# Early weight slices in tiles of their own, two transposes moved into the first feed-forward unit, and a shifted raw weight buffer

## The chip, the cores and the metric

The kernel runs on one core of a Trainium2 chip. The metric is device time in microseconds. Five engines work side by side, each strictly in the order of its own instruction list: TensorE (PE; its weight loads are listed as PEld), VectorE (DVE), ScalarE (ACT), GpSimd (POOL) and SyncE (SP), which here only issues transfers. A semaphore makes an instruction wait for one on another engine. A program places the instructions of each engine at build time, so the lists are fixed before the kernel runs.

## The reference

One transformer block on 512 positions and 2048 columns, all in float32:

```
h   = rmsnorm(x, g_attn_pre);  p = h @ w_in          # 512x2048 @ 2048x3904
o_A = stick_breaking_attention(q, k, v)              # 8 heads x 128
o_B = mla_attention(...)                             # 8 heads, low-rank q and kv
x   = x + rmsnorm(concat(rmsnorm(o_A), rmsnorm(o_B)) @ w_o, g_attn_post)
h   = rmsnorm(x, g_ffn_pre)
u   = causal_conv3(h @ w_up)                         # 2048 x 2*5632
x   = x + rmsnorm((gelu(u_gate) * u_val) @ w_down, g_ffn_post)
```

## The kernel before

Each float32 matrix is split into a high and a low part, and each product is three matmuls: high by high, high by low, low by high. A weight slice therefore passes four places: a transfer issued by SP brings it into a raw tile `wr`, ACT casts it to `wh` (L109), DVE subtracts to `wl` (L111), and TensorE reads both. Up to the feed-forward part, `load_w` (L104 to L112) does this with two raw tiles, `wr`, and four each of `wh` and `wl`.

The work around the change is at about a third of the span.

**The product with w_o.** Its columns go in four blocks of 512. Blocks c = 0, 1, 2 are done for all four row blocks of 128 positions at once (from L718). The last block is done row block by row block: `last_cols(ws, t)` (L738) is 48 matmuls of 128x512 over eight weight slices `ws`. The first four of these slices, and the first two of w_up (each 512 KB), are loaded ahead by `early_w` (L844). Its high and low parts go to pages that the feed-forward part needs only later, `a5h`, `a5l`, `a6h`, `a6l` for w_o and `a3h`, `a3l` for w_up; its raw tiles come from the same two as those of `load_w`:

```python
    def early_w(src, tag, shape):
        raw_ = new_raw(shape)
        sy.dma_start(raw_, src.rearrange("(k p) c -> p k c", p=P))
```

**The end of a row block.** After `last_cols(t)`, `residual(t)` (L779) forms the second norm and scales: DVE adds the residual (L784), ACT squares (L786), DVE sums (L754, L755), POOL raises to the power -1/2 (L757, `r`), DVE and ACT scale into `v` and `y` (L791, L793). Then `transposed(t)` (L798) turns the row block over: 16 TensorE transposes of 128x128 into four banks (L801), DVE scales each bank into a page (L803), ACT casts to `act_hi` (L774) and DVE subtracts to `act_lo` (L775). The columns of `act_hi` and `act_lo` are the positions: row blocks 0 and 1 are `lo_half`, 2 and 3 `hi_half`. In the code before, `transposed(t - 1)` stands behind `last_cols(t)`, and `transposed(3)` behind the gate's lower half.

**The first feed-forward unit.** It is done plainly: 256 gate and 256 value columns of w_up, each in four steps `kg` of 512 rows (`plain_part`, L853; matmuls at L862). Before: gate lower half, kg 0 to 3; `transposed(3)`; gate upper half, kg 0 to 3; value, kg 0 to 3, over all 512 positions. The gate slices kg 0 and 1 are the early ones. Behind it `left_sides` (L810) forms the differences of quarters of the activations (L815, L820, L821, L829).

**The units after it** go in seven products of quarters each (`sevenfold`). Their raw weight quarters are four tiles `wr` of 8 KB a partition in the pool `wq` (L982), which takes over the room of the earlier pools. DVE sums raw quarters in place (`plus`, L915), and ACT and DVE split the sums (`w_parts`, L911). A transfer into one of these tiles waits until whatever used its room before has been read.

The order of each engine's list follows the order of the code, except where a block under `issue_after` hangs on a named instruction, and where the placing program moves instructions by its own estimate of when they are ready.

Of the kernel before, what the change touches and what calls it, by code (L numbers as in the profile page):

```python
# [9 lines left out]
F32 = mybir.dt.float32  # L10
# [9 lines left out]
P = 128  # L20
S = 512
# [6 lines left out]
DFF = 5632  # L28
# [21 lines left out]
def hymba_block(ctx, tc, x, xT, positions, vecs, taps, w_in, w_uq, w_ukv, w_o, g_attn_post, w_up, w_down,  # L50
                g_ffn_post, out):
    nc = tc.nc
    te, ve, sc, po, sy = nc.tensor, nc.vector, nc.scalar, nc.gpsimd, nc.sync
# [6 lines left out]
    def stacked(name, bufs=1, side="left"):  # L60
        st = ExitStack()
        return st, st.enter_context(tc.tile_pool(name=name, bufs=bufs, side=side, reuse_waits="tile"))
# [5 lines left out]
    def bank():  # L68
        return pp.tile([P, 512], F32, tag="ps", name="ps")

    def f(t):
        return t.bitcast(F32)
# [29 lines left out]
    def new_raw(shape):  # L102
        return wp.tile(shape, F32, tag="wr", name="wr", bufs=2)

    def load_w(src, r0, kn, c0, cols):
        raw = new_raw([P, kn, cols])
        sy.dma_start(raw, src[r0:r0 + kn * P, c0:c0 + cols].rearrange("(k p) c -> p k c", p=P))
        hi = wp.tile([P, kn, cols], R32, tag="wh", name="wh")
        sc.copy(hi, raw)  # L109
        lo = wp.tile([P, kn, cols], R32, tag="wl", name="wl")  # L110
        ve.tensor_tensor(lo, raw, f(hi), ALU.subtract)  # L111
        return hi, lo  # L112
# [98 lines left out]
    def chain(*gens):  # L211
        for g in gens:
            yield from g
# [303 lines left out]
    def gen_pair(pr):  # L517
        wm[pr] = [load_w(w_ukv, 0, 2, pr * 512, 512)] + [load_w(w_uq, g * 256, 2, pr * 384, 384) for g in range(2)]
        ps = bank()
        for kk in range(4):  # L520
            wh, wl = wm[pr][1 + kk // 2]
            three(ps, wh[:, kk % 2, 256:384], wl[:, kk % 2, 256:384], cq[kk][0], cq[kk][1], kk == 0, kk == 3)
            yield 0.65
        t = rotate(ps, cos, ssin)
        rope_q[pr] = []
        for e in range(2):
            st = pg_acc(R32)
            a, b = slice(64 * e, 64 * e + 64), slice(64 - 64 * e, 128 - 64 * e)
            sc.copy(st[a, :], t[a, :])
            ve.tensor_tensor(st[b, :], t[a, :], f(st[a, :]), ALU.subtract)  # L530
            rope_q[pr].append(st)
# [3 lines left out]
    def gen_q(hd):  # L535
        pr, e = hd // 2, hd % 2
        cs_ = slice(e * 128, e * 128 + 128)
        ps = bank()
        for kk in range(4):
            wh, wl = wm[pr][1 + kk // 2]  # L540
            three(ps, wh[:, kk % 2, cs_], wl[:, kk % 2, cs_], cq[kk][0], cq[kk][1], kk == 0, kk == 3)
            yield 0.65
        q_mla[hd] = parts(ps, pg_qk)
# [77 lines left out]
    first = chain(gen_pair(0), gen_q(0), gen_q(1))  # L621
# [57 lines left out]
    tp_stack, tp = stacked("tp", side="right")  # L679
# [5 lines left out]
    def ypage(c):  # L685
        return pg_v() if c < 2 else fpage("y", 8)
# [74 lines left out]
    lo_half, hi_half = slice(0, 256), slice(256, 512)  # L761
# [5 lines left out]
    def cpage(name, shape=(8, 256), dt=R32):  # L767
        return cp.tile([P, *shape], dt, tag=name, name=name)
# [28 lines left out]
    def transposed(t):  # L797
        for c in range(4):  # L798
            ps = bank()
            for kk in range(4):  # L800
                te.transpose(ps[:, kk * P:(kk + 1) * P], y[t, c][:, kk * P:(kk + 1) * P], ident)  # L801
            raw[t, c] = ypage(c)
            ve.tensor_tensor(raw[t, c].rearrange("p (k x) -> p k x", k=4), ps.rearrange("p (k x) -> p k x", k=4),  # L803
                             g_rep[:, c, :, None].broadcast_to([P, 4, P]), ALU.mult)
            split_into(((a11, a12), (a21, a22))[t // 2][c // 2], c, t, raw[t, c])
# [33 lines left out]
    def gated(unit, m, bg, bv):  # L839
        sc.activation(bg, bg, AF.Gelu_apprx_tanh)  # L840
        ve.tensor_tensor(bg, bg, bv, ALU.mult)
        po.dma_start(g_dram[unit, :, m, :], bg)

    def early_w(src, tag, shape):  # L844
        raw_ = new_raw(shape)
        sy.dma_start(raw_, src.rearrange("(k p) c -> p k c", p=P))
        both = cpage(tag, (2, *shape[1:]))
        hi, lo = both[:, 0], both[:, 1]
        sc.copy(hi, raw_)
        ve.tensor_tensor(lo, raw_, f(hi), ALU.subtract)  # L850
        return hi, lo


    def plain_part(banks, ws, kg, hs, first):
        wh, wl = ws
        for kk in range(4):
            for m in range(2):
                ms = slice(m * P, (m + 1) * P)
                dst = banks[m][:, hs]
                ah, al = act_hi[:, 4 * kg + kk, hs], act_lo[:, 4 * kg + kk, hs]  # L860
                for i, (l, r) in enumerate(((wh, ah), (wh, al), (wl, ah))):
                    te.matmul(dst, l[:, kk, ms], r, start=first and kg == 0 and kk == 0 and i == 0,  # L862
                              stop=kg == 3 and kk == 3 and i == 2, skip_group_check=True)

    load_x2(1)
    ws = [early_w(w_o[kg * 256:(kg + 1) * 256, 1536:2048], tag, [P, 2, 512])
# [3 lines left out]
    ws += [load_w(w_o, kg * 256, 2, 1536, 512) for kg in range(4, 8)]  # L870
    for t in range(NT):
        last_cols(ws, t)
        if t > 0:
            transposed(t - 1)
        residual(t)
    ws_g += [load_w(w_up, kg * 512, 4, 0, 256) for kg in (2, 3)]
    bank_g = [bank(), bank()]
    for kg in range(4):
        plain_part(bank_g, ws_g[kg], kg, lo_half, True)
    transposed(3)  # L880
    ws_v = [load_w(w_up, kg * 512, 4, DFF, 256) for kg in range(4)]
    for kg in range(4):
        plain_part(bank_g, ws_g[kg], kg, hi_half, False)
    bank_v = [bank(), bank()]
    for kg in range(4):
        plain_part(bank_v, ws_v[kg], kg, slice(0, S), True)
    pair_g, pair_v = (tp.tile([P, 2, S], F32, tag=n, name=n, bufs=1) for n in ("ug", "uv"))
    for m in range(2):
        conv(bank_g[m], m, pair_g[:, m])
# [12 lines left out]
    wq_stack, wq = stacked("wq")  # L902

    made = []

    def w_pair(n, cols):
        return [wq.tile([P, n, cols], R32, tag=tag, name=tag, bufs=3) for tag in ("wh", "wl")]
# [10 lines left out]
    def sevenfold(quarter, shape, added=None):  # L918

        w = {}  # L920

        def p1():
            pair = w_pair(*shape)
            w[11] = quarter(0, 0)
            return w_parts(w[11], pair)

        def p2():
            w[21] = quarter(1, 0)
            return w_parts(w[21])

        def p5():
            w[12] = quarter(0, 1)
            plus(w[11], w[12])
            if added:
                added(w[12], 1, 1)
            return w_parts(w[11])

        def p6():
            w[22] = quarter(1, 1)
            parts = w_parts(plus(w[11], w[22]))  # L940
            if added:
                added(w[11], 1, 0)
            return parts

        def p7():
            return w_parts(w[12] if added else plus(w[12], w[22]))

        def p3():
            return w_parts(w[22])

        def p4():
            return w_parts(w[11] if added else plus(w[11], w[21]))

        if added:
            return p1, p2, p5, p6, p7, p3, p4
        return p1, p5, p6, p7, p2, p3, p4
# [388 lines left out]
```

## Time and profile before

| | |
|---|---|
| median of 3 runs | 2055.48 us (2050.31 to 2056.83) |
| profiled execution | 2057.59 us, its span 2055.8 us |
| granted TensorE clock, mean | 0.995 of full speed |
| TensorE busy | 2011.4 us (98%) |
| VectorE busy | 1533.4 us (75%) |
| ScalarE busy | 924.2 us (45%) |
| TensorE busy, 644 to 749 us | 99.24 us of 105.00 us |
| DMA queues | 266.12 MB, mean 129 GB/s |

How to read it: the profiled execution's own time is 1.8 us longer than its span, which begins with the first recorded instruction. The stretch from 644 to 749 us holds the last block of w_o, the row blocks' ends, and the first feed-forward unit. A timeline row gives the start of a group of like instructions and its duration. Matmuls are pipelined, and their recorded durations overlap, so the time that a run of them takes is the distance from one start to the next. The bracket at a row's end tells how long the engine was idle before it and whose instruction ended that.

### The profile page before, as it was taken

To read this page: it belongs to the slowest core of one execution; us is meant where nothing else is said; L and a number is where in the kernel's file an instruction comes from. 1 tells how busy PE (TensorE), PEld (TensorE's weight loads), DVE (VectorE), ACT (ScalarE), POOL (GpSimd) and SP (SyncE) were. 2 spreads that over 40 slices of the span, in tenths; PEclk is the share of its full clock that TensorE was granted. 3 is DMA by queue.
4 is the path that set the end of the run, shared out by engine and by line. 5 is a ranking of instruction groups with operands and counts; after the bars stand their busy time and mean duration, and the time that the engine had idled before them with its cause. 6 is when DMAs were issued, how large, how long until landed. Compare 5 with 4: busy or idle time off the path is not lost.

```text
span 2055.8 us, 29750 instructions
## 1 busy us (share of the span) xinstructions
PE 2011.4 (98%) x12532; PEld 1810.0 (88%) x12532; DVE 1533.4 (75%) x1556; ACT 924.2 (45%) x1105; POOL 160.9 (8%) x192
## 2 busy tenths in 40 slices
PE   9999999999999999999999999999999999999997
PEld 7788888888887889999999999999999788878876
DVE  7445345687234887888788888878888889898886
ACT  6334234466324644444445444444444564344432
POOL 0000000123022200000000000000000000000004
PEclk9999999999999999999999999999999999999999
DMA  8422322211434524324422432343245677667762
GB/s 265 123 79 75 94 80 63 82 42 62 139 108 144 164 93 140 107 93 133 145 93 93 158 120 93 113 156 101 93 137 182 174 207 191 195 184 171 207 196 82
DMA packets 186630, 266.12 MB, mean 129 GB/s; under 512 B 8832, under 2 KB 123648, under 8 KB 185984
## 3 DMA queue, kind: packets, MB, share of 16 engines
q1 hardware_dynamic: 170704, 227.04, 34.2%
q0 software_dynamic: 15360, 36.71, 8.1%
q8 instruction: 98, 1.61, 0.3%
q10 hardware_dynamic: 432, 0.47, 0.1%
q14 instruction: 36, 0.29, 0.0%
HBM read 244.26 MB, written 19.92 MB: 129 GB/s over the span
## 4 chain that ended last, share of the span: by engine, by line
PE 76%; DVE 11%; DMA 6%; ACT 3%; issue 3%; POOL 0%; SPq 0%; DVEq 0%; ACTq 0%; POOLq 0%
PE ps L972 40%; PE ps L120 8%; PE ps L122 8%; PE ps L121 8%; PE ps L1144 7%; DVE wl L911 3%; DMA wr<-in_w_down_dram 2%; PE ps L270 2%; PE ps L862 2%; ACT wh L911 1%; DVE wr L915 1%; DVE act_hi L1082 1%; DMA wr<-in_w_o_dram 1%; DMA acc<-in_x_dram 1%; PE ps L246 1%
## 5 line engine op out<-in xcount | busy, mean ns | idle before, releaser
L911 ACT CAST wh<-wr 128x2048 fp32r<-128x2048 f32 x220 | 418.9, 1909 | 617.7 <-DVE wr L915 280.4
L911 DVE TENSOR_TENSOR wl<-wr,wh 128x2048 fp32r<-128x2048 f32 x220 | 502.9, 2287 | 154.3 <-ACT wh L911 150.6
L972 PE MATMUL ps<-act_hi,wh 128*128 128x256 f32 x1344 | 380.4, 283 | 1.6 <-ACT wh L911 1.6
L972 PE MATMUL ps<-act_hi,wl 128*128 128x256 f32 x1344 | 380.4, 283 | 0.0
L972 PE MATMUL ps<-act_lo,wh 128*128 128x256 f32 x1344 | 380.4, 283 | 0.0
L111 DVE TENSOR_TENSOR wl<-wr,wh 128x1024 fp32r<-128x1024 f32 (+2 forms) x107 | 130.7, 1222 | 192.7 <-ACT wh L109 192.5
L972 PEld LDWEIGHTS ps<-act_hi,wh 128*128 128x128 f32 x1344 | 258.0, 192 | 1.9 <-ACT wh L911 1.8
L972 PEld LDWEIGHTS ps<-act_lo,wh 128*128 128x128 f32 x1344 | 258.0, 192 | 0.0
L972 PEld LDWEIGHTS ps<-act_hi,wl 128*128 128x128 f32 x1344 | 258.0, 192 | 0.0
L915 DVE TENSOR_TENSOR wr<-wr 128x2048 f32<-128x2048 f32 x104 | 237.7, 2286 | 1.1
L109 ACT CAST wh<-wr 128x1024 fp32r<-128x1024 f32 (+2 forms) x107 | 110.4, 1032 | 208.6 <-PE ps L121 79.8
L122 PE MATMUL ps<-wh,act_lo 128*128 128x512 f32 x400 | 156.3, 391 | 0.0
L120 PE MATMUL ps<-act_hi,wh 128*128 128x512 f32 x368 | 145.9, 396 | 0.0
L122 PE MATMUL ps<-act_hi,wl 128*128 128x512 f32 x368 | 144.1, 392 | 0.0
L120 PE MATMUL ps<-wh,act_hi 128*128 128x512 f32 x352 | 138.4, 393 | 5.7 <-ACT act_hi L194 5.1
L121 PE MATMUL ps<-act_lo,wh 128*128 128x512 f32 x368 | 143.9, 391 | 0.0
L121 PE MATMUL ps<-wl,act_hi 128*128 128x512 f32 x352 | 137.9, 392 | 1.5 <-DVE wl L111 1.5
L1144 PE MATMUL ps<-wh,act_lo 128*128 128x512 f32 x320 | 100.4, 389 | 0.9 <-DVE act_hi L1082 0.9
L972 PE MATMUL ps<-a5h,wl 128*128 128x256 f32 x336 | 95.2, 283 | 1.5 <-DVE wl L911 1.5
L972 PE MATMUL ps<-a6h,wh 128*128 128x256 f32 x336 | 95.1, 283 | 0.0
L972 PE MATMUL ps<-a5l,wh 128*128 128x256 f32 x336 | 95.1, 283 | 0.0
L972 PE MATMUL ps<-a6h,wl 128*128 128x256 f32 x336 | 95.1, 283 | 0.0
(392 smaller groups left out, 4344.1 us busy)
## 6 DMA issues: line engine op xcount, KB each, us to landing
wr<-in_w_up_dram SPq DMA_DIRECT2D x84, 1024.0 KB, 7.0
wr<-in_w_down_dram SPq DMA_DIRECT2D x44, 1024.0 KB, 6.9
wr<-in_w_in_dram SPq DMA_DIRECT2D x59, 512.0 KB, 3.8
wr<-in_w_down_dram POOLq DMA_DIRECT2D x20, 1024.0 KB, 9.7
wr<-in_w_o_dram SPq DMA_DIRECT2D x32, 512.0 KB, 3.6
g_dram<-v POOLq DMA_DIRECT2D x42, 256.0 KB, 5.9
a5l<-g_dram SPq DMA_DIRECT2D x5, 1024.0 KB, 11.1
a5h<-g_dram SPq DMA_DIRECT2D x5, 1024.0 KB, 8.2
```

Source lines behind the costliest of these rows:

```text
L109: sc.copy(hi, raw)
L111: ve.tensor_tensor(lo, raw, f(hi), ALU.subtract)
L120: te.matmul(ps, lh, rh, start=start, stop=False)
L121: te.matmul(ps, lh, rl, start=False, stop=False)
L122: seen["mm"] = te.matmul(ps, ll, rh, start=False, stop=stop)
L246: te.transpose(dst, a(b, j), ident)
L270: te.matmul(dst, q[:, b * P:(b + 1) * P], k[:, k0:S], start=i == 0, stop=False)
L862: te.matmul(dst, l[:, kk, ms], r, start=first and kg == 0 and kk == 0 and i == 0, stop=kg == 3 and kk == 3 and i == 2, skip_group_check=True)
L911: made.append((sc.copy(hi, w), ve.tensor_tensor(lo, w, f(hi), ALU.subtract)))
L915: ve.tensor_tensor(w, w, v, ALU.add)
L972: te.matmul(dst, l[:, k, ms], r[:, k, :], start=fresh and k == 0 and m == 0 and i == 0, stop=k == 7 and i == 2, skip_group_check=True)
L1144: te.matmul(bs[t], l[:, k, ts_], r[:, k, :], start=fresh and k == 0 and i == 0, stop=k == FU - 1 and i == 2, skip_group_check=True)
```

## The change

Three edits.

1. The six early slices take their raw tiles from `ug` and `uv`, two tiles of the pool `tp` that the first unit later uses for its gate and value pages, in turn.
2. `transposed(2)` moves from behind `last_cols(3)` to behind the gate's lower half kg 1, and `transposed(3)` from behind the gate's lower half to behind the value's lower half kg 0. So that there is work for TensorE, the value's steps kg 0 and 1 are now done in two halves of 256 positions, the lower one ahead of the gate's upper half. The last two value slices are loaded later in the code.
3. A tile `gap` of 1 KB a partition is taken in `wq` before the first raw quarter, which moves the four raw places up by 1 KB.

```diff
     def early_w(src, tag, shape):
-        raw_ = new_raw(shape)
+        halves.append(tp.tile(shape, F32, tag=("ug", "uv")[len(halves) % 2], name="wr", bufs=1))
+        raw_ = halves[-1]
...
     for t in range(NT):
         last_cols(ws, t)
-        if t > 0:
+        if 0 < t < 3:
             transposed(t - 1)
         residual(t)
     ws_g += [load_w(w_up, kg * 512, 4, 0, 256) for kg in (2, 3)]
     bank_g = [bank(), bank()]
     for kg in range(4):
         plain_part(bank_g, ws_g[kg], kg, lo_half, True)
-    transposed(3)
-    ws_v = [load_w(w_up, kg * 512, 4, DFF, 256) for kg in range(4)]
+        if kg == 1:
+            with tc.issue_after(mark["part"].ins):
+                transposed(2)
+    ws_v = [load_w(w_up, kg * 512, 4, DFF, 256) for kg in range(2)]
+    bank_v = [bank(), bank()]
+    plain_part(bank_v, ws_v[0], 0, lo_half, True)
+    with tc.issue_after(mark["part"].ins):
+        transposed(3)
+    plain_part(bank_v, ws_v[1], 1, lo_half, True)
+    ws_v += [load_w(w_up, kg * 512, 4, DFF, 256) for kg in (2, 3)]
     for kg in range(4):
         plain_part(bank_g, ws_g[kg], kg, hi_half, False)
-    bank_v = [bank(), bank()]
     for kg in range(4):
-        plain_part(bank_v, ws_v[kg], kg, slice(0, S), True)
+        plain_part(bank_v, ws_v[kg], kg, hi_half if kg < 2 else slice(0, S), False)
...
         def p1():
             pair = w_pair(*shape)
+            if not made:
+                wq.tile([P, 256], F32, tag="gap", name="gap", bufs=1)
             w[11] = quarter(0, 0)
```

`mark["part"]` is the last matmul that `plain_part` issued. In the code after, `early_w` and `plain_part` stand 3 lines lower (L846 is L849, L862 is L865), and the lines from L911 on 10 and more lower.

**SP, the loads of w_o.** In the list before, the six early loads (L846) stand behind the last load of block c = 2 (L107, first row here) and ahead of the four other slices of the last block:

```order
L107 DMA wr_5192<-in_w_o_dram 128x2x512
L846 DMA wr_5246<-in_w_o_dram 128x2x512
L846 DMA wr_5251<-in_w_o_dram 128x2x512
L846 DMA wr_5256<-in_w_o_dram 128x2x512
L846 DMA wr_5261<-in_w_o_dram 128x2x512
L846 DMA wr_5266<-in_w_up_dram 128x4x256
L846 DMA wr_5271<-in_w_up_dram 128x4x256
L107 DMA wr_5276<-in_w_o_dram 128x2x512
L107 DMA wr_5282<-in_w_o_dram 128x2x512
```

In the list after, the same place has the last block's other slices right behind those of c = 2:

```order
L107 DMA wr_5162<-in_w_o_dram 128x2x512
L107 DMA wr_5192<-in_w_o_dram 128x2x512
L107 DMA wr_5276<-in_w_o_dram 128x2x512
L107 DMA wr_5282<-in_w_o_dram 128x2x512
L107 DMA wr_5288<-in_w_o_dram 128x2x512
L107 DMA wr_5294<-in_w_o_dram 128x2x512
```

The six early loads (now L849) have gone up among the first four of the 14 loads of the blocks c = 0 to 2, two ahead of them, two behind the second, and two behind the fourth:

```order
L849 DMA wr_5246<-in_w_o_dram 128x2x512
L849 DMA wr_5251<-in_w_o_dram 128x2x512
L107 DMA wr_4750<-in_w_o_dram 128x2x512
L107 DMA wr_4780<-in_w_o_dram 128x2x512
L849 DMA wr_5256<-in_w_o_dram 128x2x512
L849 DMA wr_5261<-in_w_o_dram 128x2x512
L107 DMA wr_4832<-in_w_o_dram 128x2x512
L107 DMA wr_4862<-in_w_o_dram 128x2x512
L849 DMA wr_5266<-in_w_up_dram 128x4x256
L849 DMA wr_5271<-in_w_up_dram 128x4x256
```

**TensorE, behind the last matmul of `last_cols(3)`.** L122 is that matmul, L801 the transposes of row block 2, L862 the first matmuls of the gate's lower half. Before:

```order
L122 MATMUL ps<-wh,act_lo 128x512
L801 MATMUL ps<-ident,v 128x128 x8
L801 MATMUL ps<-ident,y 128x128 x8
L862 MATMUL ps<-act_hi,a3h 128x256
L862 MATMUL ps<-act_lo,a3h 128x256
```

After, at the same place, and then at the end of the gate's lower half kg 1 (`a3l`), 34 rows on:

```order
L122 MATMUL ps<-wh,act_lo 128x512
L865 MATMUL ps<-act_hi,a3h 128x256
L865 MATMUL ps<-act_lo,a3h 128x256
...
L865 MATMUL ps<-act_hi,a3l 128x256
L801 MATMUL ps<-ident,v 128x128 x8
L801 MATMUL ps<-ident,y 128x128 x8
L865 MATMUL ps<-act_hi,wh 128x256
```

The 16 transposes have left the place behind the last block of w_o; 48 matmuls now stand ahead of them.

**DVE, around the pages of `transposed(3)`** (the second L803 of two `v` is its first). Before, with L791 and L815, L820 of `left_sides` ahead of it:

```order
L815 TENSOR_TENSOR y<-v,y 128x512
L791 TENSOR_SCALAR v<-x_5518,r_5762 128x512
L791 TENSOR_SCALAR y<-x_5522,r_5762 128x512
L815 TENSOR_TENSOR y<-v,y 128x512
L820 TENSOR_TENSOR v<-v 128x512
L775 TENSOR_TENSOR a5l<-y,a5h 128x4x128 x2
L803 TENSOR_TENSOR v<-ps,gv 128x512 x2
L803 TENSOR_TENSOR y<-ps,gv 128x512
L775 TENSOR_TENSOR act_lo<-v,act_hi 128x4x128 x2
```

After, with the last operations on the pages of row block 2 (L803, L775 `act_lo`) between L791 and that place:

```order
L791 TENSOR_SCALAR y<-x_5522,r_5726 128x512
L775 TENSOR_TENSOR act_lo<-v,act_hi 128x4x128
L803 TENSOR_TENSOR y<-ps,gv 128x512
L775 TENSOR_TENSOR act_lo<-y,act_hi 128x4x128
L111 TENSOR_TENSOR wl<-wr,wh 128x1024
L775 TENSOR_TENSOR act_lo<-y,act_hi 128x4x128
L815 TENSOR_TENSOR y<-v,y 128x512 x2
L820 TENSOR_TENSOR v<-v 128x512
L775 TENSOR_TENSOR a5l<-y,a5h 128x4x128 x2
L821 TENSOR_TENSOR v<-v,y 128x512
L803 TENSOR_TENSOR v<-ps,gv 128x512 x2
L775 TENSOR_TENSOR act_lo<-v,act_hi 128x4x128 x2
```

## Rows read from the trace of the kernel before

**Rows 1.** The page's first part: busy us (share) and instructions of each engine.
```profile
PE 2011.4 (98%) x12532; PEld 1810.0 (88%) x12532; DVE 1533.4 (75%) x1556; ACT 924.2 (45%) x1105; POOL 160.9 (8%) x192
```

**Rows 2.** Waits of PE, 640 to 800 us: total, times, longest.
```profile
PE ps L801 <- ACT v L793: 3.2, 2, 2.9
PE ps L972 <- ACT wh L911: 1.6, 1, 1.6
PE ps L121 <- DVE wl L111: 1.5, 2, 0.8
PE ps L972 <- DVE wl L911: 1.5, 1, 1.5
```

**Rows 3.** Timeline of PE: starts of last_cols(0), last_cols(1), transposes: start, us.
```profile
643.78 0.39 PE L120 MATMUL ps<-a5h,act_hi 128*128 128x512 f32 x1
...
657.83 0.40 PE L120 MATMUL ps<-a5h,act_hi 128*128 128x512 f32 x1
...
668.73 1.03 PE L801 MATMUL ps<-ident,v 128*128 128x128 f32 x8
```

**Rows 4.** Timeline of SP's queue, 612 to 660 us: the early loads, then the others.
```profile
619.11 12.72 SPq L846 DMA_DIRECT2D wr<-in_w_o_dram  x4
...
640.11 10.42 SPq L107 DMA_DIRECT2D wr<-in_w_o_dram  x4
```

**Rows 5.** Timeline of PE around transposed(1) and transposed(2), [idle before <-releaser].
```profile
681.85 1.09 PE L801 MATMUL ps<-ident,v 128*128 128x128 f32 x8 [0.28 <-ACT v L793]
...
683.58 0.48 PE L120 MATMUL ps<-a5h,act_hi 128*128 128x512 f32 x1
...
694.36 0.39 PE L122 MATMUL ps<-wh,act_lo 128*128 128x512 f32 x1
697.63 1.26 PE L801 MATMUL ps<-ident,v 128*128 128x128 f32 x8 [2.88 <-ACT v L793]
...
700.25 0.56 PE L862 MATMUL ps<-act_hi,a3h 128*128 128x256 f32 x1
```

**Rows 6.** Windows: us; PE, PEld, DVE, ACT, POOL busy; PEclk; DMA; GB/s.
```profile
697.60:700.20 2.60, 2.57 (x16) 2.57 (x17) 2.52 (x7) 2.14 (x3) 0.54 (x1) 0.66 0.55 173
...
716.00:727.00 11.00, 11.00 (x92) 11.00 (x93) 10.91 (x18) 4.72 (x7) 0.00 (x0) 1.00 0.10 32
```

**Rows 7.** Timeline of PE, transposed(3) to the upper half, 711.9 to 716.5 us.
```profile
712.54 1.04 PE L801 MATMUL ps<-ident,v 128*128 128x128 f32 x8
...
714.79 0.50 PE L862 MATMUL ps<-act_hi,a3h 128*128 128x256 f32 x2 [0.34 <-ACT act_hi L774]
715.13 0.64 PE L862 MATMUL ps<-act_hi,wh 128*128 128x512 f32 x2
...
716.15 0.28 PE L862 MATMUL ps<-act_hi,a3h 128*128 128x256 f32 x1
```

**Rows 8.** Timeline of POOL, 694 to 712 us: the power for residual(3).
```profile
698.74 0.54 POOL L757 TENSOR_TENSOR r<-s,nhalf 128x1 f32<-128x1 f32 x1 [1.92 <-DVE s L755]
```

**Rows 9.** Timeline of DVE, 692 to 716 us: one row of each kind.
```profile
703.92 1.41 DVE L784 SCALAR_TENSOR_TENSOR x<-v,r,x 128x512 f32<-128x512 f32 x2
...
706.57 1.22 DVE L111 TENSOR_TENSOR wl<-wr,wh 128x1024 fp32r<-128x1024 f32 x1
...
710.19 0.49 DVE L791 TENSOR_SCALAR v<-x,r 128x512 f32<-128x512 f32 x1 [0.45 <-POOL r L757]
...
712.19 1.29 DVE L775 TENSOR_TENSOR a5l<-y,a5h 128x512 fp32r<-128x512 f32 x2
713.39 1.28 DVE L803 TENSOR_TENSOR v<-ps,gv 128x512 f32<-128x512 f32 x2
```

**Rows 10.** Waits of SP's queue, 600 to 760 us.
```profile
SPq L982 <- DVE a3l L775: 27.4, 1, 27.4
```

**Rows 11.** Timeline of DVE where the first unit ends and the next begins.
```profile
743.46 2.29 DVE L911 TENSOR_TENSOR wl<-wr,wh 128x2048 fp32r<-128x2048 f32 x1 [3.55 <-issue]
748.98 0.75 DVE L836 SCALAR_TENSOR_TENSOR uv<-ps,gvc,uv 128x511 f32<-128x511 f32 x1 [3.23 <-ACT uv L835]
749.64 2.28 DVE L915 TENSOR_TENSOR wr<-wr 128x2048 f32<-128x2048 f32 x1
```

More of the change, by code (lines that the diff above doesn't have):

```diff
@@ L842, in gated @@
         po.dma_start(g_dram[unit, :, m, :], bg)
+    mark, halves = {}, []
     def early_w(src, tag, shape):
-        raw_ = new_raw(shape)
+        halves.append(tp.tile(shape, F32, tag=("ug", "uv")[len(halves) % 2], name="wr", bufs=1))
+        raw_ = halves[-1]
         sy.dma_start(raw_, src.rearrange("(k p) c -> p k c", p=P))
@@ L861, in plain_part @@
                 for i, (l, r) in enumerate(((wh, ah), (wh, al), (wl, ah))):
-                    te.matmul(dst, l[:, kk, ms], r, start=first and kg == 0 and kk == 0 and i == 0,
-                              stop=kg == 3 and kk == 3 and i == 2, skip_group_check=True)
+                    mark["part"] = te.matmul(dst, l[:, kk, ms], r, start=first and kg == 0 and kk == 0 and i == 0,
+                                             stop=kg == 3 and kk == 3 and i == 2, skip_group_check=True)
     load_x2(1)
```

## The prediction

> **What bounds the kernel now.** I read the busy shares first: TensorE is busy for 98% of the span [rows 1], so almost nothing can be won but the little that it waits, and work added to it is paid in full. Next I read its waits in the stretch that the change touches [rows 2]. There are four kinds worth naming: the transposes wait for the scaled row block (3.2 us, 2.9 of it once), the last block of w_o waits for `wl` (1.5), and the first seven-product unit waits twice, for `wl` (1.5) and `wh` (1.6). The timelines then say which of them the three edits reach. `last_cols(0)` runs from 643.78 to 657.83, 14.05 us, where the same 48 matmuls of `last_cols(1)` take 10.90, or 0.227 us each [rows 3]. The reason is in SP's list: the six early slices go out from 619.11 on through the same two raw tiles, and the other four slices of the block start only at 640.11 [rows 4], a few us before they are wanted. The 2.88 us stand ahead of `transposed(2)`: the last matmul of `last_cols(3)` starts at 694.36, the first transpose at 697.63 [rows 5].
>
> **What is taken away.** All in TensorE time, since it has nothing to do beside it.
> - The late slices: 14.05 - 10.90 = 3.15 us. With the six early ones loaded among the first of c = 0 and into other tiles, the four late ones stand directly behind those of c = 2, two at a time in their ring. I count all of it.
> - The wait ahead of `transposed(2)`: 697.63 - 694.36 - 0.227 = 3.04 us [rows 5]. The gate's lower half uses row blocks 0 and 1 alone, which have long been turned over, so it can start at once.
> - The slow clock behind that wait. [...] The 96 matmuls of the gate's lower half follow, from 700.25 to 712.54 [rows 5, 7], 12.29 us; at 11.00/92 = 0.120 us each [rows 6] they would take 11.52. That is 0.77 more.
> - The waits behind `transposed(3)`: its first transpose starts at 712.54 and at 1.73 for the 16 it would be done by 714.27, but the upper half runs freely only from 716.15 [rows 7], 1.88 later. Five matmuls were done in between, three of 128x256 and two of 128x512, 3 x 0.120 + 2 x 0.227 = 0.81. The rest, 1.07, goes.
>
> Sum: 3.15 + 3.04 + 0.89 + 0.77 + 1.07 = 8.92 us.
>
> **What is added.** Two steps of the value (kg 0 and 1) are done in halves: 48 matmuls of 128x512 become 96 of 128x256, and each pair costs 2 x 0.120 - 0.227 = 0.013 us more: 0.62 us. [...]
>
> Then there is a new wait, not shown before. The first matmuls of the gate's upper half need `act_hi` and `act_lo` of row block 3, and DVE makes the latter. I count from the start of the last matmul of `last_cols(3)`, 694.36. TensorE has ahead of the upper half: that matmul, 0.227; 96 matmuls of the gate's lower half, 11.52; 48 of the value's lower half, 5.76; two times 16 transposes, 3.46; and 0.12 to the first that needs `act_lo`. It arrives after 21.1 us. DVE must first have r for `residual(3)`, ready at 698.74 + 0.54 [rows 8], 4.9 us after 694.36; that chain hangs on the same matmul as before. From there its list runs in order: four of L784 in 706.57 - 703.92 = 2.65; two of L111 at 1.22, 2.44; 18 operations of 128x512 on two operands (seven L803, seven L775, four of L815, L820 and L821) at (713.39 - 712.19)/2 = 0.60, 10.8; two of L791 at 0.49, 0.98 [rows 9]. That makes 16.9, and I add 0.7 for its waits on ACT and POOL (one such wait of 0.45 stands in [rows 9]) and four one-column operations. So `act_lo` is there after 4.9 + 16.9 + 0.7 = 22.5 us, and TensorE waits 1.4, in two pieces: a first for `act_hi` and the rest for `act_lo`. Bounds: 0, if placing and overlap give DVE 1.4 us back; 3.04, the wait of the same kind that [rows 5] shows. I take 1.4, with 0.1 for the restart, 1.5.
>
> The moved loads: on SP the six stand ahead of the second load of c = 0 and wait for casts of their own tiles, so the first slices of c = 0 could come late. Their ACT and DVE work is 6 casts and 6 subtractions that are only done earlier, on engines that have room there (VectorE 75%, ScalarE 45% [rows 1]). I count nothing; each slice that came late would cost about what one did in `last_cols(0)`, 3.15/3 = 1.05. The gap moves raw places but no work on an engine.
>
> The first seven-product unit: I count nothing. In the kernel before SP's queue stood 27.4 us at a raw quarter whose place waited for the last `a3l` [rows 10]. In the list after, the quarter that is needed for the first sum no longer does, and comes about that much earlier. But the sum itself (L915, 749.64) stands on DVE right behind the value's L836 (748.98), which waited 3.23 us, through ACT, for the last matmul of the plain unit [rows 11]. The quarter can be early and the sum still starts with the end of the plain unit, so the waits of 1.5 and 1.6 stay.
>
> **The sum.** -8.92 + 0.62 + 1.5 = -6.8 us: 2050.8 against the profiled execution's 2057.59, which lies 2.1 above the median. Against the median of 2055.48 it is 2048.7. Two measurements of this kernel can be told apart from about 0.3%, 6.2 us.
>
> **Rivals.**
> 1. The new wait costs more (chance 0.18). A wait of 2.88 us was followed by a slow clock [rows 5, 6], and a new one in two pieces may be too: that gives back 0.89 + 0.77 = 1.66, and a longer wait, up to the bound of 3.04, 1.5 more. Then -6.8 + 3.2 = -3.6, 2051.9. Against it: the two waits of 1.5 and 1.6 [rows 2] stand in stretches at the full clock on both sides. [...]
> 2. The early loads don't save anything (0.10): the four slices of the last block wait for `wh` and `wl` places that TensorE frees at its own pace, or the loads of c = 0 come late by as much. Then the 3.15 us are lost: -3.7, 2051.8. For it: the change puts six loads among the first of c = 0, just when TensorE needs those. Against it: the others had their raw place only from 640.11.
> 3. The first unit's two waits go as well (0.12), if what released them was the quarter after all: -6.8 - 3.1 = -9.9, 2045.6. For it: 27.4 us of waiting leave SP's queue. Against it: the order on DVE in [rows 11].
> 4. Slower (0.06): DVE becomes the bound of the upper half. Its list now has everything of row blocks 2 and 3 and a part of `left_sides` ahead of the pages of `transposed(3)`. If its queue runs so late that `act_lo` comes 8.3 us or more behind TensorE (the 1.5 counted and the 6.8 won), nothing is left; with 3 us more, and the slow clock behind it, 1.66, the time is 2060. From [rows 9] DVE would need half its work again for that.
>
> The forecast itself has 0.54, with its own range of 2046.5 to 2051; its middle lies just past the 6.2 us, so I give three fifths of it to faster. With rival 3 and a small part of the others that is 0.32 + 0.12 + 0.03 = 0.47 faster; 0.47 no difference; 0.06 slower. The range for 8 in 10 takes in rivals 1, 2 and most of 3: 2044.8 to 2053.5.
>
> **What would show it.** In the profile after: `last_cols(0)` of about 10.9 us without a wait for `wl`; no idle time ahead of the gate's lower half and full clock there; one short wait, for `act_hi` and `act_lo`, at the gate's upper half, 1 to 2 us; the two waits of the first unit as before, with the raw quarters landed long ahead. It would be wrong if waits for `wl` come up at the start of c = 0, if the clock falls at the upper half, or if the unit's first waits are gone.

## The result, and the profile after

The changed kernel took 2041.44 us (median of 5 runs, 2040.72 to 2043.86), the kernel before 2054.09 in the same comparison: a ratio of 0.9947, with a 95% interval of 0.9934 to 0.996. Two later comparisons gave 0.9957 (0.9945 to 0.9969) and 0.9949 (0.9936 to 0.9961). So the change saves about 10 us, 8.8 to 10.9 by the three ratios. (The ratio is not simply that of the two medians, which lie 12.7 us apart in the first comparison; I go by the ratios.) I had forecast 6.8 with a range down to 2044.8; it was faster, as forecast, and by more than the range allowed. In the two later comparisons the changed kernel's medians are 2045.33 and 2044.70, at the edge of that range, so the size of the miss is partly that of one comparison; the saving by the ratio is above 6.8 in all three.

In the changed kernel's profile (2040.72 us, span 2038.9) the stretch of the change looks as forecast. First TensorE's waits from 630 to 800 us; the columns are those of [rows 2]:

```profile
PE ps L984 <- ACT wh L921: 1.6, 1, 1.6
PE ps L984 <- DVE wl L921: 1.5, 1, 1.5
PE ps L865 <- DVE act_lo L775: 0.8, 1, 0.8
PE ps L801 <- ACT v L793: 0.3, 1, 0.3
```

Of [rows 2], the wait of the transposes has shrunk from 3.2 to 0.3, the wait for the late slices (1.5) is gone, the two waits of the first seven-product unit stand as they were, and 0.8 for `act_lo` is new. In TensorE's timeline, where [rows 3], [rows 5] and [rows 7] were read:

```profile
639.95 0.39 PE L120 MATMUL ps<-a5h,act_hi 128*128 128x512 f32 x1
...
650.83 0.39 PE L120 MATMUL ps<-a5h,act_hi 128*128 128x512 f32 x1
...
687.32 0.39 PE L122 MATMUL ps<-wh,act_lo 128*128 128x512 f32 x1
687.54 0.28 PE L865 MATMUL ps<-act_hi,a3h 128*128 128x256 f32 x1
...
708.34 0.38 PE L865 MATMUL ps<-act_hi,a3h 128*128 128x256 f32 x1
709.48 0.39 PE L865 MATMUL ps<-act_lo,a3h 128*128 128x256 f32 x1 [0.76 <-DVE act_lo L775]
```

`last_cols(0)` takes 650.83 - 639.95 = 10.88 us, the gate's lower half begins 0.22 us after the last matmul of `last_cols(3)`, and at the upper half there is one wait. The windows of that stretch (columns of [rows 6]) show the full clock throughout:

```profile
687.50:699.10 11.60, 11.60 (x99) 11.56 (x99) 9.86 (x21) 8.07 (x19) 3.85 (x7) 1.00 0.63 201
708.30:717.30 9.00, 8.24 (x68) 8.01 (x67) 9.00 (x16) 3.65 (x7) 0.00 (x0) 1.00 0.45 143
```

On DVE, the rows that set that wait are the list that I had added up, in the order shown ahead of the prediction:

```profile
706.34 0.69 DVE L821 TENSOR_TENSOR v<-v,y 128x512 f32<-128x512 f32 x1
706.94 1.29 DVE L803 TENSOR_TENSOR v<-ps,gv 128x512 f32<-128x512 f32 x2
708.14 0.68 DVE L803 TENSOR_TENSOR y<-ps,gv 128x512 f32<-128x512 f32 x1
708.74 1.29 DVE L775 TENSOR_TENSOR act_lo<-v,act_hi 128x512 fp32r<-128x512 f32 x2
```

DVE has no idle time in these rows: `act_lo` is ready when its queue comes to it, at about 709.4.

Where the time went, by stages of TensorE, in every profile of the two kernels (us). "Stretch" is from the first matmul of `last_cols(0)` to the first of the seven-product units, 643.78 to 748.64 in the first profile; "units" from there to the first down product; "down" from there to the last matmul. "Down waits" are TensorE's waits in it, summed from the view of waits.

| profile | rows 0 and 1 of the last columns | stretch | units | down | down waits |
|---|---|---|---|---|---|
| before, first | 26.62 | 104.87 | 850.32 | 445.67 | 14.1 |
| before, `same` | 29.26 | 108.56 | 850.33 | 443.95 | 13.0 |
| before, `look2` | 26.95 | 105.47 | 850.32 | 444.49 | 12.5 |
| before, `look3` | 27.25 | 105.34 | 850.32 | 441.40 | 12.3 |
| before, `look4` | 26.83 | 105.34 | 850.32 | 444.43 | 13.2 |
| after, first | 23.42 | 97.69 | 850.32 | 439.91 | 12.0 |
| after, `after_again` | 23.42 | 97.67 | 850.30 | 441.34 | 10.6 |
| after, `after_third` | 23.43 | 97.69 | 850.32 | 442.75 | 11.0 |

The stretch gives 7.2 us between the two first profiles, 7.7 between the medians (105.34 and 97.69), 8.2 between the means (105.92 and 97.68). In the changed kernel it is the same to 0.02 us each time; in the kernel before it varies by 3.7. The units are equal. Down differs by 3.1 between the medians, with the same instructions in the same order. What comes before the stretch differs between executions of the same kernel too (its first matmul starts at 641.2 to 646.0 us before, 640.0 to 642.4 after); that is the program's start, not the change.

### The profile page after: what moved, and what is told of

Its sections match the earlier page's. It is cut to its first block, busy times and chain, and to the rows that moved or that the text cites. A ratio compares the mean times of both kernels' runs of the same rounds, so it can differ in the third digit from the quotient of the medians.

```text
span 2038.9 us, 29849 instructions
## 1 busy us (share of the span) xinstructions
PE 2003.2 (98%) x12580; PEld 1808.4 (89%) x12580; DVE 1532.6 (75%) x1556; ACT 924.4 (45%) x1105; POOL 159.6 (8%) x192
## 4 chain that ended last, share of the span: by engine, by line
PE 82%; DVE 9%; DMA 3%; issue 3%; ACT 3%; POOL 0%; SPq 0%; DVEq 0%; ACTq 0%; POOLq 0%
PE ps L984 40%; PE ps L1156 10%; PE ps L120 9%; PE ps L121 9%; PE ps L122 9%; PE ps L270 2%; DVE wl L921 2%; ACT wh L921 1%; DMA wr<-in_w_down_dram 1%; PE ps L865 1%; DVE wr L925 1%; PE ps L246 1%; DVE act_hi L1094 1%; DVE t L452 0%; DVE wl L111 0%
## 5 line engine op out<-in xcount | busy, mean ns | idle before, releaser
L122 PE MATMUL ps<-wh,act_lo 128*128 128x512 f32 x400 | 156.2, 390 | 0.0
L122 PE MATMUL ps<-act_hi,wl 128*128 128x512 f32 x368 | 143.4, 390 | 0.0
L984 PE MATMUL ps<-a5h,wh 128*128 128x256 f32 x336 | 95.1, 283 | 0.0
L984 PE MATMUL ps<-a3h,wh 128*128 128x256 f32 x336 | 95.1, 283 | 0.0
```

Source lines behind the costliest of these rows:

```text
L122: seen["mm"] = te.matmul(ps, ll, rh, start=False, stop=stop)
L984: te.matmul(dst, l[:, k, ms], r[:, k, :], start=fresh and k == 0 and m == 0 and i == 0, stop=k == 7 and i == 2, skip_group_check=True)
```

## The experiments

**Repeat, and each edit taken back.** `same` is the kernel before unchanged. `no_gap`, `no_early` and `no_moves` are the changed kernel without one edit:

```diff
  no_gap:    -  wq.tile([P, 256], F32, tag="gap", name="gap", bufs=1)
  no_early:  -  raw_ = halves[-1]  (tiles "ug", "uv")
             +  raw_ = new_raw(shape)
  no_moves:  the code before from load_x2(1) to bank_v, value undivided
```

> The kernel before, unchanged, for a second profile. In the two profiles shown, the last block of w_o to the first unit accounts for 7.4 us of the 16.9 us between the spans; 3.6 us come before 61 us and 5.9 us after 1600 us, where the code is the same. Theory A (those 9.5 us are not made by the change: transfers and clock differ from one execution to the next): this second profile differs from the first by 2 us or more in the start or after 1600 us, and at least one of the clock's drops at 56.7 and 1964.8 us is absent or elsewhere. Theory B (the change itself works on the later parts): the second profile repeats the first to within 1 us in both places, with both drops.

> The changed kernel without the 1 KB tile. The first sum of the first seven-product unit stands on the vector engine behind the value's convolution, so an earlier raw quarter should not matter: by theory A the same time as the changed kernel, within 1.5 us, and the two waits of 1.5 and 1.6 us as before. Theory B, with the shifted raw places as the cause: 3 to 5 us slower than the changed kernel, in the down products.

> The changed kernel with the six early slices in the two raw tiles of load_w again. Theory A and my prediction: the three waits in the first row block of the last columns come back, 3.2 us, and the time is 3.2 us above the changed kernel. Rival: the clock also changes nothing, but the loads among those of c = 0 cost something there, so it loses less than 2 us.

> The changed kernel with the transposes of row blocks 2 and 3 back in their places and the value undivided. My prediction: 3.04 + 0.89 + 0.77 + 1.07 come back, less the 0.62 of the split and the measured new wait of 0.8, so 4.2 us above the changed kernel, with the drop of the clock at about 690 us. Theory B: more than 8 us, because the lower clock or later phase also reaches the end.

`same` took 2054.21 us, a ratio of 0.9996 (0.9985 to 1.0007). Its profile is longer than the first by 3.7 us in the stretch and shorter by 1.7 in down, and its clock fell in other places: theory A for the variation. The lower clock stands at the waits of `last_cols(0)`, where the first profile had none. Windows over the first two row blocks, of the first profile and then of `same`:

```profile
643.80:657.80 14.00, 11.91 (x49) 8.83 (x48) 7.99 (x7) 7.45 (x13) 7.00 (x4) 1.00 0.47 152
657.80:670.40 12.60, 12.60 (x66) 10.63 (x64) 7.07 (x15) 6.05 (x15) 3.56 (x6) 1.00 0.51 176
```

```profile
641.20:656.50 15.30, 13.11 (x50) 9.66 (x49) 8.11 (x8) 7.48 (x13) 6.91 (x4) 0.87 0.51 156
656.50:670.40 13.90, 13.90 (x64) 11.56 (x63) 7.01 (x15) 6.12 (x15) 3.58 (x6) 0.89 0.45 156
```

The engine waited about as long in both (2.1 and 2.2 us in all), but with a granted clock of 0.87 and 0.89 the two row blocks took 2.6 us more. The rest of the 3.7, about 1 us, lies behind `transposed(2)`, where the clock is lower for longer than in the first profile (0.50 from 698.4 to 701.8 us in that one); more on that below, under `fillers`.

`no_gap`: 2043.25 us, ratio 0.9938 (0.9921 to 0.9954), stretch 97.74, and the first unit's waits are 1.6 and 1.5 as in the changed kernel. `no_early`: 2046.66 us, 0.9953 (0.9936 to 0.9971), stretch 101.31: 3.6 us come back there. `no_moves`: 2050.07 us, 0.9975 (0.9965 to 0.9985), stretch 101.96: 4.3 us come back there, as expected, but 8.6 in the medians, which are of two comparisons. The changed kernel's own median is 2041.44, 2045.33 and 2044.70 in three of them, so medians of different comparisons can't be set against each other to better than 4 us. In the same comparison stands `no_gap`, which is the changed kernel but for a tile that gives nothing alone (next group). Against it, `no_early` is 3.4 us slower by the medians and 3.1 by the ratios, and `no_moves` 6.8 and 7.6, where the stretch gives 4.2; their profiles differ by 2.0 in down too (442.12 and 444.11).

**Each edit alone**, beside the changed kernel on one chip.

> The changed kernel once more, beside single edits on one chip. The stretch from the last block of w_o to the first unit took 97.7 us in its first profile, 104.9 and 108.6 in two profiles of the kernel before; the second of these had a clock drop at the waits of the first row block too. Theory A (what is beyond the 7 us is the clock, which falls after some waits in some executions and not in others): this profile has 97.7 us again in the stretch, and may have drops at about 1600 and 1950 us that the first did not have, so it is up to 3 us longer there. Theory B (the change works on the down products): they take 365.3 us again, where the kernel before took 369.7 and 368.7.

> The kernel before with the 1 KB tile alone. Theory A: the time of the kernel before within 1.5 us, the first unit's two waits of 1.5 and 1.6 us stay, and in the stretch 104.9 us or 108.6, as the clock falls or not at the first row block. Theory B with the raw places: down products of 365 to 367 us and 2 to 4 us less.

> The kernel before with the early slices in tiles of their own alone. My sum: 3.2 us less. Theory A: 3.2 to 6.5 us less in the runs, since the drop of the clock at these waits goes as well, 1.7 to 3.4 us in the executions that had it; the stretch takes 101.7 to 102. Rival: no more than 3.2, the clock's cost in the median unchanged.

> The kernel before with the moved transposes alone, value in halves. My sum: 4.2 us less with the measured new wait of 0.8. Theory A: 4.2 to 7.6 us less, as the drop behind the wait of 2.9 us lasts 3.4 us in some executions and 6.8 in others; the stretch takes 101.3 us, or up to 3.4 more if the clock falls at the first row block. Rival: over 8 us, as the undoing of this edit cost 8.6 in the changed kernel, which would mean that it also shortens something after 1600 us.

Against 2054.10 for the kernel before: `after_again` 2045.33 us (ratio given above), `only_gap` 2055.53 (1.0008, 1.0 to 1.0017), `only_early` 2050.57 (0.9982, 0.9974 to 0.9991), `only_moves` 2048.22 (0.9972, 0.9962 to 0.9982). In us by the ratios: +1.6, -3.7 and -5.7, together -7.8, to -8.8 for all three at once. Within their intervals the edits add up, and the 1 KB tile gives nothing alone. `only_early` has 1.8 to 5.3 us by its interval, which doesn't separate theory A from the rival; `only_moves` has 3.7 to 7.8, inside theory A and short of the rival's 8. The stretch took 109.03, 101.91 and 101.79 us. `only_gap` shows the drop at the first row block too, with 29.83 us for row blocks 0 and 1, and `only_moves`, which has the late slices as well, with 27.53.

**Filling the waits instead of removing them.** `fillers` is the kernel before with spare matmuls at both places, `fill_first` with those in the first row block alone.

```diff
 # last_cols
+            if t == 0 and k_ in (12, 14):
+                spare = bank()
+                for i in range(4):
+                    te.matmul(spare, mix[0][0][:, 0, 0:P], ws[5][0][:, 0, :], start=i == 0, stop=i == 3)
 # the loop over t, behind last_cols(3); fillers only
+            spare = bank()
+            for i in range(12):
+                te.matmul(spare, mix[0][0][:, 0, 0:P], ws[7][0][:, 0, :], start=i == 0, stop=i == 11)
```

> The kernel before with spare matmuls of 128x512 where TensorE waits: four ahead of each of the last two slices of the first row block, twelve (2.7 us) ahead of transposed(2); their results are not read, and what is waited for comes no sooner. Theory A (beyond the waits themselves, the clock behind them is what the change won): no lower clock near 652 and 697 us, a stretch of 103 to 104 us where the kernel before had 104.9 to 109.0, and 2 to 5 us less time for 20 matmuls more. Rival (the clock is none of it, the difference lies in the waits alone): the stretch keeps its 104.9 to 109.0 and the time does not change.

> The kernel before with spare matmuls in the first row block of the last columns alone: four of 128x512 ahead of each of the last two slices, their result not read. The slices come no sooner; only the idle time there is filled. Theory (the drop of the clock behind these waits, in two of three profiles of this code, is what my sum left out): first and second row block take 26.6 us together as in the first profile, never 29.3 to 29.8, and the time in the runs is 1.5 to 3 us below the kernel before. Rival (the difference is made elsewhere, after 1600 us): 26.6 us, but no difference in the time.

`fillers`: 2055.37 us, 1.0003 (0.9994 to 1.0012): no gain, against theory A. The clock stayed up at both places (1.00 from 643.8 to 668.7 us and from 697.0 to 712.5), and yet the stretch took 106.39 us. These are the rival's numbers, but not for its reason. The timeline of TensorE shows why, first at the transposes of row block 2, then of 3:

```profile
695.25 1.09 PE L805 MATMUL ps<-ident,v 128*128 128x128 f32 x8 [0.17 <-ACT v L797]
696.18 1.04 PE L805 MATMUL ps<-ident,y 128*128 128x128 f32 x8
...
712.51 0.50 PE L866 MATMUL ps<-act_hi,a3h 128*128 128x256 f32 x2 [1.85 <-ACT act_hi L778]
```

The 16 transposes (696.98 - 695.25 = 1.73 us) and the lower half (1.00 in the windows) ran at the full clock, and TensorE then waited 1.85 us at the upper half, where [rows 7] has 0.34. The upper half started 20.54 us after the last matmul of `last_cols(3)`, in the kernel before 714.79 - 694.36 = 20.43. What sets it there is the chain of residual, transposes and DVE; the slow clock ahead of it was hidden. A profile of the unchanged kernel, `look3`, shows the same without any spare matmul. The clock is at 1.00 behind the wait of 2.90 us, and TensorE waits at the upper half instead, which starts 716.32 - 696.04 = 20.28 us after the last matmul of `last_cols(3)`. First a window behind the wait, then the timeline:

```profile
699.30:702.70 3.40, 3.37 (x30) 3.38 (x31) 3.37 (x9) 2.81 (x4) 0.54 (x1) 1.00 0.40 127
```

```profile
696.04 0.39 PE L122 MATMUL ps<-wh,act_lo 128*128 128x512 f32 x1
699.33 1.09 PE L801 MATMUL ps<-ident,v 128*128 128x128 f32 x8 [2.90 <-ACT v L793]
...
716.32 0.51 PE L862 MATMUL ps<-act_hi,a3h 128*128 128x256 f32 x2 [1.77 <-ACT act_hi L774]
```

Only where the clock stayed down longer, in `same` and `only_gap`, did some of it show: the first matmul that needs `act_lo` starts 22.6 us after that last matmul there, 21.4 to 21.9 in the other profiles with the transposes in their old places.

In `fillers` the clock then fell behind the new wait, and that was not hidden:

```profile
697.00:700.40 3.40, 3.40 (x30) 3.40 (x29) 3.40 (x6) 2.63 (x6) 0.58 (x1) 1.00 0.25 95
713.70:717.10 3.40, 3.40 (x16) 3.40 (x17) 3.40 (x6) 1.66 (x3) 0.00 (x0) 0.50 0.23 76
```

`fill_first`: 2053.64 us, 0.9995 (0.9987 to 1.0004). Row blocks 0 and 1 took 26.96 us with no drop, as expected, but the time did not move by the 1.5 to 3 us: the drop there is too rare in the kernel before to count for so much in its median. Three further profiles of the kernel before say so too.

> The kernel before, a third profile. Theory: the first and second row block take 26.6 us where the clock stays up and 29 to 30 where it falls; over the profiles the mean lies between, near 28.5. Rival: 26.6 us is the rule, and the two profiles with more were exceptions.

> The kernel before, a fourth profile, for the same count: 29 to 30 us in the two row blocks by the theory, more often than 26.6.

> The kernel before, a fifth profile, for the same count: 29 to 30 us in the two row blocks by the theory, more often than 26.6.

They took 26.95, 27.25 and 26.83 us there. Against my theory, 26.6 to 27.3 is the rule and the drop is the exception: one in five profiles of the kernel before, three in eight with the variants that have the same late slices (`only_gap` and `only_moves` with it, `no_early` without). But the first profile was the shortest of the five, by 0.2 to 0.6 us without a drop.

**The first unit's waits.** In `values_later` the value's convolution hangs on the second pair of weight parts:

```diff
-        with tc.issue_after(made[0][0].ins), tc.issue_after(made[0][1].ins):
+        with tc.issue_after(made[1][0].ins), tc.issue_after(made[1][1].ins):
             for m in range(2):
                 conv(bank_v[m], NFF + m, pair_v[:, m])
```

> The changed kernel with the value's convolution of the first unit hung on the second pair of weight parts, not the first, so that on the vector engine two sums of raw quarters (L925) stand ahead of it. The quarter for the first sum lands at 712.9 us in the changed kernel, long before. Theory: the two waits of the first unit are set by the vector engine's order; the one of 1.46 us goes, and the one of 1.63 shrinks or goes: 1.5 to 3 us less than the changed kernel in the first unit. Rival: it only moves the work, and the wait comes back at the next products: no change.

> The same without the 1 KB tile. The quarter for the first sum lands only about 740 us, after the plain unit's end. Theory: now the 1 KB matters: the first unit waits as long as before or longer (3 us or more), 1.5 to 4 us slower than with the tile. Rival: the tile still makes no difference, within 0.5 us in the first unit.

> The changed kernel a third time, beside the three others on one chip. 97.7 us in the stretch again and the first unit with its waits of 1.5 and 1.6 us; after 1600 us 365 to 369 us for the down products, as the clock falls there or not. In the time 7 to 11 us below the kernel before, with the middle near 9: the stretch gives 7.2 where the kernel before keeps its clock at the first row block and 11 where it does not.

On one chip: `after_third` 2044.70 us, `values_later` 2040.76 (0.9934 of the kernel before, 0.9922 to 0.9946), `values_later_no_gap` 2046.13 (0.9961, 0.995 to 0.9973). The waits of TensorE in the first unit, with the tile and then without it:

```profile
PE ps L984 <- DVE wl L921: 0.5, 1, 0.5
```

```profile
PE ps L982 <- DVE wl L921: 3.0, 1, 3.0
```

With the tile the units take 847.71 us for 850.32, without it 851.56. On DVE the two sums follow at once with the tile, and each waits for its transfer without it:

```profile
736.78 4.62 DVE L925 TENSOR_TENSOR wr<-wr 128x2048 f32<-128x2048 f32 x2
```

```profile
738.50 2.29 DVE L925 TENSOR_TENSOR wr<-wr 128x2048 f32<-128x2048 f32 x1 [2.09 <-DMA wr<-in_w_up_dram]
742.65 2.29 DVE L925 TENSOR_TENSOR wr<-wr 128x2048 f32<-128x2048 f32 x1 [1.85 <-DMA wr<-in_w_up_dram]
```

The reason is the second raw quarter. Its issue in the queue of SP, in the changed kernel and in `no_gap` (there with the third):

```profile
703.96 0.52 SPq L994 DMA_DIRECT2D wr<-in_w_up_dram  x1
```

```profile
734.52 0.99 SPq L992 DMA_DIRECT2D wr<-in_w_up_dram  x2
```

So the 1 KB lets the quarter go 30.6 us earlier (28.7 if counted from the first raw quarter, which goes at 703.49 and 705.30), and that is worth nothing as long as the sum that needs it stands behind the value's convolution on DVE. With both, the units are 2.6 us shorter than in the changed kernel, as expected; in the runs the intervals of `values_later` and `after_third` overlap (0.9946 and 0.9936), so there the gain is likely but not shown. Without the tile `values_later_no_gap` is 5.4 us slower by the medians, above the 1.5 to 4 expected, and 3.9 in the units.

**Is the rest a matter of when?** `after_late` is the changed kernel with 40 spare matmuls in the plain unit:

```diff
+    spare = bank()
+    for i in range(40):
+        te.matmul(spare, mix[0][0][:, 0, 0:P], ws_v[0][0].rearrange("p a b -> p (a b)")[:, 0:512], start=i == 0, stop=i == 39)
     for kg in range(4):
         plain_part(bank_v, ws_v[kg], kg, hi_half if kg < 2 else slice(0, S), False)
```

> The changed kernel with 40 spare matmuls of 128x512 (40 x 0.227 = 9.1 us, result not read) in the plain unit, so that all that follows comes as late as in the kernel before. In profiles TensorE waits 12.3 to 14.1 us after the first down product in the kernel before and 10.6 to 12.0 in the changed one, for the same instructions. Theory C (it hangs on how late the program reaches that part): 12.3 to 14.1 us again, and a time 9.1 + 1 to 3 us above the changed kernel, so the kernel before's. Theory D (it hangs on the code or its places): 10.6 to 12.0 us, and 9.1 us above the changed kernel, about 1 us below the kernel before. Theory A (chance of the few profiles): either.

It took 2054.06 us (0.9995, 0.9985 to 1.0005), 8.7 to 12.6 above the medians of the changed kernel, and the stretch 106.77, 9.1 more. In its profile TensorE waits, after the first down product:

```profile
PE ps L1159 <- DVE wl L924: 5.5, 3, 2.9
PE ps L1159 <- DVE act_hi L1097: 5.4, 7, 1.1
PE ps L1159 <- ACT act_hi L1095: 1.6, 2, 1.0
PE ps L1159 <- ACT wh L924: 0.3, 1, 0.3
```

That is 12.8 us, at the lower end of theory C, but one profile, where those of the same kernel differ by 1.4 to 1.8. The time is 1.0 us below the kernel before by the ratio, theory D's figure, with an interval that holds theory C's too. It doesn't decide.

All nineteen profiles together say more. Ten are of kernels with the transposes in their old places (the five before, `only_gap`, `only_early`, `no_moves`, `fillers`, `fill_first`), nine of kernels with the moved ones (the three after, `no_gap`, `no_early`, `only_moves`, `values_later`, `values_later_no_gap`, `after_late`).

| | transposes in old places, 10 profiles | transposes moved, 9 profiles |
|---|---|---|
| down, median (us) | 444.5 | 442.4 |
| down, range (us) | 441.4 (`look3`), then 443.6 to 446.3 | 439.6 to 442.8 |
| last long wait for `wl`, about 363 us into down, median (us) | 2.76 | 2.13 |
| mean granted clock over the 10 us from that wait's start | 0.66 in seven, 0.83 in two, 1.00 in `look3` | 0.83 in eight, 1.00 in one |

So down is about 2 us shorter with the transposes moved, whatever the other two edits do, and on each of the three chips that ran both kinds; `look3` is the one exception. Most of it lies at one place: from the start of that wait to the 60th matmul behind it the medians are 19.9 and 18.4 us. The windows there in the first profile before and in `after_again`:

```profile
1962.50:1972.50 10.00, 6.59 (x17) 4.84 (x17) 7.96 (x8) 1.90 (x1) 0.00 (x0) 0.66 0.88 273
```

```profile
1951.20:1961.20 10.00, 7.29 (x24) 5.59 (x25) 7.96 (x6) 1.90 (x1) 0.00 (x0) 0.83 0.77 254
```

How late the program gets there doesn't sort the profiles: `no_moves` and `only_early` begin down at 1593.0 and 1593.4 us and take 444.11 and 443.63, `no_early` and `only_moves` begin it at 1593.1 and take 442.57 and 439.61, and `after_late`, at 1598.4, takes 442.65. Why two transposes moved at about 690 us bear on a wait at about 1960 us no run shows.

## Why the prediction was wrong

In the stretch the steps came out, though one of them for another reason than mine (below): 104.87 to 97.69 is 7.18 us between the two profiles, where the steps gave 6.8.

- The late slices: 3.15 forecast, 14.05 - 10.88 = 3.17 found against the first profile.
- From the last matmul of `last_cols(3)` to the first seven-product matmul: 3.04 + 0.89 + 0.77 + 1.07, less 0.62 and 1.5, is 3.65; found 54.28 - 50.32 = 3.96 (748.64 - 694.36 before, 737.64 - 687.32 after). The upper half's first matmul that needs `act_lo` starts 709.48 - 687.32 = 22.16 us after the last of `last_cols(3)`, where I had 22.5. The row shows 0.76 of idle time in one piece, not 1.4 in two: ACT had `act_hi` in time. The 0.1 for the restart came: the matmul behind the one at 709.48 starts at 709.70, 0.22 us later, where the free run has 0.120.
- The first unit's waits stayed, against rival 3, because DVE's list sets them: forecast, and shown by `values_later`.
- Rival 2 is out: the 462 matmuls ahead of `last_cols(0)`, among which the early loads go out (540.6 to 560.8 us), take 104.86 us without a wait in both first profiles, and `only_early` keeps its gain. Rival 1 did not come: after the wait of 0.76 the clock stayed at 1.00. Nor did rival 4: DVE did not become the bound by more than that.

What failed is the step "the sum": a sum made on the stretch of one profile was carried over to the median of the runs, with nothing for what the clock and the transfers do from one execution to the next, and nothing, without a reason given, for the program behind the stretch.

1. The term of the late slices was mis-sized for the median. The same rows of the kernel before, in five profiles, are 26.62, 26.83, 26.95, 27.25 and 29.26 us, against 23.42 after: 3.2 to 5.8, with a middle of 3.5 and a mean of 4.0. The sum rested on the smallest, and in one of five the clock fell behind those waits. With the whole stretch that makes 7.7 (medians) to 8.2 us (means) instead of 7.2. The three waits of up to 0.8 us were taken as their own length; I had asked whether the clock follows a wait for the new one alone, not for those that go.
2. The down products were left out. In the eight profiles of the two kernels their part is shorter by 3.1 us in the median, 2.0 of it in the waits (13.0 and 11.0), but the two groups overlap (442.75 after, 441.40 before). Over all nineteen profiles it is 2.0 us and goes with the moved transposes, most of it at one wait and the lower clock behind it. So of about 10 us, 8 are found in the stretch and about 2 in down; how the move brings about the latter stays open.

One reading in the sum was right in its total and wrong in its parts. I took 1.66 us for the slow clock behind the wait of 2.88 us (0.50 from 698.4 to 701.8 us): 0.77 on the gate's lower half, and 0.89 on the 16 transposes of `transposed(2)`, which take 700.25 - 697.63 = 2.62 us, where those of `transposed(1)` take 683.58 - 681.85 = 1.73 [rows 5]; the same 1.73 stands for 16 transposes in the other sums. `fillers` and `look3` show that this clock alone gives nothing, since the upper half waits for the chain of `residual(3)` through DVE in both kernels; by the same chain the 2.88 us alone would have given nothing either, which no run tests. The chain is nearly as long in both: from the last matmul of `last_cols(3)` to the free run of the upper half it is 716.15 - 694.36 = 21.79 us before and 709.48 - 687.32 = 22.16 after. What the change did is to put 48 more matmuls, 5.76 us of work, into this time. The sum of idle times came to nearly the same because all of the idle time up to that point was in it.

The range was too narrow for this: it had ends for the new wait and the first unit, and none for the execution that the profile happened to catch, nor for anything behind the stretch.

## What to carry to other kernels

Take the term that a sum rests on from more than one execution where waits stand there that the clock may follow: the same 48 matmuls with the same late slices took 14.05 to 15.30 us. Where an engine stands idle ahead of a point that another engine's chain sets, ask how much work fits in front of that point; filling a wait, or winning back a slow clock ahead of it, is worth nothing if the chain ends last anyway: `fillers`, with the clock at 1.00 behind the filled wait, has a ratio of 1.0003, and in `look3`, at 1.00 there too, the upper half still starts 20.28 us after the last matmul of `last_cols(3)`, for 20.43 in the first profile. An earlier transfer paid here only where the instruction that uses it was not queued behind another wait: the 1 KB tile was worth nothing alone and 5.4 us by the medians (2046.13 to 2040.76), 3.9 of it in the units, once the list on DVE was put right. Last, a part of the program that the change doesn't touch can still differ with it: compare it over many profiles, grouped by edit, before counting it as nothing.

## What the runs showed of the hardware

After the same wait, in the same code, the granted clock falls in one execution and not in another. Some 13 us after the first down product TensorE waits 2.85 to 2.9 us for `wl` in every profile. In the first profile of the kernel before the clock stays up behind it, at 1.00, in `same` it is at 0.50 of full speed:

```profile
1614.60:1618.00 3.40, 3.37 (x15) 2.80 (x16) 2.89 (x2) 1.07 (x1) 0.00 (x0) 1.00 1.02 419
```

```profile
1615.20:1618.60 3.40, 2.83 (x7) 2.26 (x8) 3.37 (x3) 0.53 (x1) 0.00 (x0) 0.50 1.02 420
```

The second of these stretches begins 0.6 us before the wait ends. Behind the wait the matmuls start 0.23 us apart in the one profile and 0.43 in the other. Behind the waits of 1.5 and 1.6 us in the first unit the first profiles of the two kernels have no such drop (1.00 from 748.6 to 768.0 us before, from 740.0 to 758.0 after), and the units take 850.30 to 850.33 us in all eight profiles of the two; behind a wait of 1.7 us in `last_cols(0)` there is one in `same` (0.87 over 641.2 to 656.5 us). In these runs, whether the drop comes can't be told from the length of the wait alone.
